# Hybrid decoder layer on one core: where weight splits and decays are computed, and in which order

## The chip, the cores and the metric

The kernel runs on one core of one Trainium2 chip. The core has a matrix engine (TensorE, PE in the profile), three engines for element-wise work (VectorE = DVE, ScalarE = ACT, GpSimd = POOL), and SyncE (SP), whose queue issues most DMA transfers. Each engine works through its own list of instructions in a fixed order and waits where an instruction's inputs or output slot are not ready. The metric is the device time of one execution in microseconds, the median over runs: 1209.37 us before the change.

## The reference

The program is one layer of a decoder, for 1024 tokens of width 1024, in float32:

```
h = rmsnorm(x); proj = h @ w_in
q,k,v (4 heads of 128) = silu(causal_conv4(proj_qkv));  q,k = l2norm(q), l2norm(k)
g = -exp(a_log) * softplus(a + dt_bias);  beta = sigmoid(b);  gc = cumsum(g)
o_a = gated delta rule over chunks (decays exp(gc_t - gc_j), triangular solve, state carried)
o_a = rmsnorm(o_a) * silu(z)
o_b = dilated sliding-window attention, 8 heads of 64, three (window, dilation) branches merged
x = x + concat(o_a, o_b) @ w_out
x = x + (silu(gate) * up) @ w_down, with gate, up = causal_conv3(rmsnorm(x) @ w_up)
return rmsnorm(x)
```

Products are computed in three passes: each float32 operand is split into a high part in TensorE's fast format and the low part that is left, and hi x hi, hi x lo and lo x hi are added up. So every weight needs a split before it is used: a copy that rounds (whi) and a subtraction (wlo = weight - whi).

## The kernel before, in words

The Python program emits instructions stream by stream. A small planner, the class `Weave` (L49), keeps a modelled clock of TensorE and of the other engines; each stream is a generator that says after how long it wants to go on, and among those that are due the one with the lowest level is taken. So the order of the products on TensorE is fixed when the program is written (`mm` stamps it, L193). On the other engines a scheduler orders the instructions: by readiness in its own timeline, and among ready ones by the order of emission. The wrappers `ve`, `ac`, `po_` (L151 to L156) emit to VectorE, ScalarE and GpSimd; `uv` and `ua` do so with a priority ahead of what was emitted before (`URGENT`). `after(inst, anchor)` (L189) adds an ordering alone. All element-wise work that goes through these wrappers has the line L142 in the profile, or L144 with priority.

`first()` computes three key heads. `dense()` (L494) then walks the rest of the input projection, one weight of 128 x 1024 after the other: the fourth key (list index 0), four plus four pieces for the values (1 to 8), then query and value tiles head by head (9 to 16), the attention's tiles (17 to 24), the gates z (25 to 28). `take()` (L512) hands out the weight for now, emits the split of the next one and the load of the one behind it. Raw weights (wst), high parts (whi) and low parts (wlo) have two slots each. `weight()` (L215) splits: those with index 1 to 8 in two halves of 512 columns with priority, the others whole and without.

`values_by_token` (L521) fills four banks with a group of the values, which ScalarE copies out into vx (L536); the next group uses the same banks. For each key, `conv_silu` (L457) runs the causal filter (a copy and a tanh on ScalarE, three filter steps and a last multiplication on VectorE), and `kprep(h)` (L598) the preparation of the delta rule: it loads the rows of gc into dec, masks them on GpSimd, takes eight exponentials on ScalarE (the decays, L613), has the key transposed into tokens and squared (`tokens`, L579, with priority on ScalarE), multiplies the key with itself and forms um from products, bp and dec (L641). From um of all keys VectorE solves small triangular systems by substitution (`forward_sub`, L684), whose blocks are merged on TensorE (`merges`); then come the chains of the four heads (`chain`), attention, output projection and the MLP. GpSimd takes powers of -0.5 and 0.5 for norms, some masks and fills, copies of reciprocals (rd), and the scaling of the heads' outputs (vtok by ms, L863).

Of the kernel before, what the change touches and what calls it, by code (L numbers as in the profile page):

```python
# [147 lines left out]
def hybrid_layer(tc, I, out):  # L148
# [23 lines left out]
    def A(name, tag, dt=F32, shape=(P, 1024)):  # L172
        if tag in TURNS:
            i = turns[tag] = turns.get(tag, -1) + 1
            tag = TURNS[tag][i % len(TURNS[tag])]
        return tile_(lp, shape, dt, name, tag, SLOTS[tag])
# [12 lines left out]
    def after(inst, anchor, reason="keeps a slot free until it is needed"):  # L189
        tc.add_manual_dep(inst.ins, anchor.ins.name, order, reason=reason)  # L190
# [9 lines left out]
    def mm3(dst, lhs, rhs, first, last, **kw):  # L200
# [2 lines left out]
        mm(dst, lhs[0], rhs[1], us, False, False, **kw)  # L203
        mm(dst, lhs[1], rhs[0], us, False, last, **kw)

    def split(src, hi, lo):
        ac.activation(hi, src, AF.Copy)
        return ve.tensor_tensor(lo, src, hi.bitcast(F32), op=OP.subtract)

    def raw_weight(src, n=1024):  # L210
# [1 line left out]
        sy.dma_start(st, src)  # L212
        return st

    def weight(src, n=1024, st=None, urgent=False):  # L215
        if st is None:
            st = raw_weight(src, n)
        hi = tile_(wp, [P, n], F32R, "whi", "whi", 2)
        lo = tile_(wp, [P, n], F32R, "wlo", "wlo", 2)
        for sl in (half(0), half(1)) if urgent else (slice(0, n),):  # L220
            (ua if urgent else ac).activation(hi[:, sl], st[:, sl], AF.Copy)
            (uv if urgent else ve).tensor_tensor(lo[:, sl], st[:, sl], hi[:, sl].bitcast(F32), op=OP.subtract)
        return hi, lo

    def wk_by_halves(src):
# [43 lines left out]
    def half(i):  # L269
        return slice(i * 512, i * 512 + 512)  # L270

    def v8(t):
        return t.rearrange("p (c t) -> p c t", c=NCH)
# [220 lines left out]
    def dense():  # L494

        yield from wv.until("first")
        yield from wv.until("norms")
        wv.add(2, first_keys())

        srcs, tiles = [], 0  # L500
        for col in DENSE:
            if col[0] == "V":
                srcs += [I["wv"][j] for j in range(4)]
            else:
                srcs.append(I["wi"][tiles])
                tiles += 1
        place = [0]
        raw = [raw_weight(srcs[0])]
        nxt = [weight(None, st=raw.pop())]
        raw.append(raw_weight(srcs[1]))  # L510

        def take():  # L512
            w = nxt.pop()
            i = place[0] = place[0] + 1
            if i < len(srcs):
                nxt.append(weight(None, st=raw.pop(), urgent=1 <= i <= 8))
            if i + 1 < len(srcs):
                raw.append(raw_weight(srcs[i + 1]))
            return w

        def values_by_token(g):  # L521

            banks = [bank(t) for t in ("asc", "asc", "ch", "ch")]
            for j in range(4):
                w = [t.rearrange("p (k m) -> p k m", k=2) for t in take()]
                for kk in range(2):
                    k = 2 * j + kk
                    for i, pt in enumerate(banks):
                        c = 4 * g + i
                        yield wv.need(pt, *w)  # L530
                        mm3(pt, [t[:, c * P:(c + 1) * P] for t in xs[k]], [t[:, kk, :] for t in w], k == 0, k == KT - 1)
            for i in range(0, 4, 2):
                vx = A("vx", "ev", shape=(P, 2, 512))
                for e in range(2):
                    c = 4 * g + i + e
                    ac.activation(vx[:, e, :], banks[i + e], AF.Copy, scale=rst[:, c:c + 1])  # L536
                c = 4 * g + i
                sy.dma_start(vpark[c * P:(c + 2) * P].rearrange("(e p) d -> p e d", e=2), vx)
            wv.done.add(("V", g))

        for i, col in enumerate(DENSE):
            kind, h = col[:2]
            if kind == "V":
                yield from values_by_token(h)
                continue
            if kind == "z":
                yield from wv.until(("o", h))
            w = [t.rearrange("p (k m) -> p k m", k=KT) for t in take()]
            pair = []
            for hh in range(2):  # L550
                pt = bank("hf")
                yield wv.need(pt, *w)
                for k in range(KT):
                    mm3(pt, [t[:, k, :] for t in w], [t[:, half(hh)] for t in xs[k]], k == 0, k == KT - 1)
                    yield 0.0

                pair.append(pt)
                if hh == 0:
                    xr = A("aqkv" if kind == "a" else "xr", "go" if kind == "k" else "ev")
                scaled(pair, "xr", kind == "a", t=xr, hs=(hh,))  # L560
            if kind == "k":
                T["k", h] = conv_silu(xr, 4 + h, "kT", "kT*")
                wv.add(3, kprep(h))
            elif kind == "q":
                q = conv_silu(xr, h, "qT", "qa")
                wv.add(4, qprep(h, q))
            elif kind == "v":
                v = conv_silu(xr, 8 + h, "vT", "qa")
                wv.add(4, vprep(h, v))
            elif kind == "z":  # L570
                og = gated[h] = A("og", "kT*")
                sy.dma_start(og, mixer[h])
                ve.tensor_tensor(og, og, silu2(xr, "zz"), op=OP.mult)
            else:
                sy.dma_start(apark[h, col[2]], xr)
                wv.done.add(col)
        wv.done.add("dense")
# [20 lines left out]
    def kprep(h):  # L598
        d = G[h]
        kT = T["k", h]  # L600
        yield from wv.until("gates")
        yield wv.need(gc)

        dec = A("dec", ("dv", "dw")[h % 2])
        gend = small("gend")
        gel = small("gel")
        rows = gdram.rearrange("(c h) t -> h c t", h=H)[h]
        sy.dma_start(v8(dec), bass.AP(tensor=rows.tensor, offset=rows.offset, ap=[[0, P]] + list(rows.ap)))
        po_.affine_select(v8(dec), v8(dec), pattern=[[0, NCH], [1, P]], compare_op=OP.is_ge, fill=NEG,
                                base=0, channel_multiplier=-1)  # L610
        late = "the rows may come later than the keys"
        after(ve.tensor_copy(gel, v8(dec)[:, :, P - 1]), kends[h][1], late)
        for c in range(NCH):  # L613
            inst = ac.activation(v8(dec)[:, c, :], v8(dec)[:, c, :], AF.Exp, bias=ngc[:, c, h:h + 1])
            after(inst, kends[h][0], late)
        ve.tensor_tensor(gend, gel, gc[:, :, h], op=OP.subtract)
        eg = small("eg")
        ac.activation(eg, gend, AF.Exp)
        ge = small("ge", 4)
        ac.activation(ge, gel, AF.Exp)  # L620
        yield wv.need(kT, slack=SLACK + 1.5 * (h == 0))
        ssk = small("ssk")
        d["ktok"] = yield from tokens(kT, A("ktok", "kt"), None, ssk)
        ve.tensor_scalar(ssk, ssk, 4.0 * EPS, None, op0=OP.add)
        nk = small("nk", 4)
        po_.tensor_tensor(nk, ssk, phalf, op=OP.pow)
        bp = small("bp", 4)
        ve.reciprocal(bp, ssk)
        ve.tensor_tensor(bp, bp, beta[:, :, h], op=OP.mult)
        ke = small("ke", 4)  # L630
        ve.tensor_tensor(ke, bp, eg, op=OP.mult)

        um = A("um", "uy", shape=(P, NCH, P))
        for c0 in range(0, NCH, 4):
            pt = yield from next_bank("atr", slack=KSLACK * (c0 == h == 0))
            for c in range(4):
                cs = slice((c0 + c) * P, (c0 + c + 1) * P)
                mm(pt[:, c * P:(c + 1) * P], kT[:, cs], kT[:, cs], 0.215)
            for c in range(4):
                i = c0 + c  # L640
                ve.scalar_tensor_tensor(um[:, i, :], pt[:, c * P:(c + 1) * P], bp[:, i:i + 1],  # L641
                                               dec[:, i * P:(i + 1) * P], op0=OP.mult, op1=OP.mult)
        md = mdram[h].rearrange("(c r) (j i) -> r j c i", r=4, j=32)
        for r in range(4):
            b = slice(32 * r, 32 * r + 32)
            sy.dma_start(md[r], um[b, :, b])
        d.update(kT=kT, dec=dec, ge=ge, nk=nk, bp=bp, ke=ke, um=um)
        wv.done.add(("k", h))
        if all(("k", i) in wv.done for i in range(H)):
            forward_sub()  # L650
# [411 lines left out]


    ots = {}
    last = {}
    x1 = {}
    MORDER = (0, 4, 1, 5, 2, 6, 3, 7)

# [576 lines left out]
```

## Time and profile before

| what | value |
|---|---|
| median of 3 runs | 1209.37 us (1208.98 to 1209.37) |
| profiled execution, its own time | 1209.18 us |
| its span, first to last instruction | 1207.4 us |
| TensorE busy | 1192.3 us (99%) |
| VectorE / ScalarE / GpSimd busy | 925.8 / 576.2 / 59.1 us |
| granted TensorE clock, mean | 0.996 |

The times in a row are microseconds from the start of the span, then the duration; ps, whi, wlo, dec, vx, um are the program's names of tiles (out<-in). A bracket at the end of a row is the idle time of the engine before it and what ended it. TensorE's products overlap, so their spacing from start to start is what counts, not the duration of one.

### The profile page before, as it was taken

What the parts mean: (1) busy time and instruction counts of PE and PEld (TensorE: products, weight loads), DVE (VectorE), ACT (ScalarE), POOL (GpSimd) and SP (SyncE); (2) the same over time, 40 slices, a digit from 0 to 9 for tenths busy, and PEclk for the clock granted to TensorE, in tenths of its full rate; (3) what the DMA queues carried; (4) which work ended last, traced back from release to release, by engine and by line L of the source; (5) the groups of instructions that cost most, each with busy time, mean ns of one, the idle gap of its engine ahead of it and who ended that gap; (6) DMA issues with size and microseconds to landing.
All of it is one profiled execution on the core that took longest, in us unless ns stands there. A gap on an engine that the chain in (4) does not pass through costs nothing.

```text
span 1207.4 us, 18350 instructions
## 1 busy us (share of the span) xinstructions
PE 1192.3 (99%) x7068; PEld 986.6 (82%) x7068; DVE 925.8 (77%) x1470; ACT 576.2 (48%) x1134; POOL 59.1 (5%) x78
## 2 busy tenths in 40 slices
PE   9999999999999999999999999999999999999997
PEld 7887888889877778888888888888888888888886
DVE  7683975666466556768988989889898889999865
ACT  7384335356355443655545445444454454444441
POOL 0211010003211000000000000000000000000000
PEclk9999999999999999999999999999999999999999
DMA  7424343435633213544223132231322298556513
GB/s 230 111 75 125 117 120 108 157 102 167 213 118 119 89 36 100 174 136 157 71 69 105 53 105 82 75 105 53 105 65 93 89 366 311 177 163 226 162 57 140
DMA packets 85798, 154.80 MB, mean 128 GB/s; under 512 B 21168, under 2 KB 36304, under 8 KB 85712
## 3 DMA queue, kind: packets, MB, share of 16 engines
q1 hardware_dynamic: 85136, 153.12, 39.3%
q8 instruction: 55, 0.90, 0.3%
q10 hardware_dynamic: 576, 0.52, 0.1%
q14 instruction: 31, 0.25, 0.1%
HBM read 117.68 MB, written 35.93 MB: 127 GB/s over the span
## 4 chain that ended last, share of the span: by engine, by line
PE 93%; DVE 3%; ACT 2%; issue 1%; DMA 1%; SPq 0%; POOLq 0%; POOL 0%; DVEq 0%; ACTq 0%
PE ps L193 44%; PE pa L193 20%; PE dw L193 17%; PE pc L193 10%; PE ps L197 3%; DVE kT L142 1%; DMA xt<-in_xT 1%; DVE wlo L142 0%; ACT dec L142 0%; DVE xr L142 0%; DVE x1h L142 0%; PE pd L193 0%; DVE qT L142 0%; SPq L142 0%; ACT xr L142 0%
## 5 line engine op out<-in xcount | busy, mean ns | idle before, releaser
L193 PE MATMUL dw<-pr 128*128 128x512 f32 (+1 forms) x984 | 211.3, 376 | 0.0
L193 PEld LDWEIGHTS dw<-pr 128*128 128x128 f32 x984 | 176.7, 188 | 33.6
L193 PE MATMUL ps<-xhi,whi 128*128 128x512 f32 x384 | 157.3, 410 | 0.0
L193 PE MATMUL ps<-xlo,whi 128*128 128x512 f32 x384 | 150.0, 391 | 0.8 <-DVE xlo L142 0.8
L193 PE MATMUL ps<-xhi,wlo 128*128 128x512 f32 x384 | 150.2, 391 | 0.0
L193 PE MATMUL pa<-T,pair 128*128 128x512 f32 x528 | 127.0, 389 | 0.0
L193 PEld LDWEIGHTS pa<-T,pair 128*128 128x128 f32 x528 | 99.0, 188 | 20.5
L193 PEld LDWEIGHTS ps<-xhi,whi 128*128 128x128 f32 x384 | 72.2, 188 | 18.1 <-issue 4.7
L193 PEld LDWEIGHTS ps<-xhi,wlo 128*128 128x128 f32 x384 | 72.1, 188 | 15.7 <-DVE wlo L142 0.2
L193 PEld LDWEIGHTS ps<-xlo,whi 128*128 128x128 f32 x384 | 72.4, 188 | 13.4 <-DVE xlo L142 1.1
L142 ACT ACTIVATE u<-pa 128x512 f32<-128x512 f32 x44 | 26.3, 598 | 107.3 <-PE pa L193 107.3
L142 DVE SCALAR_TENSOR_TENSOR y<-xu,fcw,y 128x1023 f32<-128x1023 f32 (+1 forms) x44 | 56.4, 1281 | 22.1 <-ACT y L142 22.0
L142 ACT ACTIVATE whi<-wst 128x1024 fp32r<-128x1024 f32 (+2 forms) x33 | 33.3, 1009 | 68.0 <-PE ps L193 62.4
L193 PE MATMUL pa<-B,A 128*128 128x512 f32 x264 | 63.4, 389 | 0.0
L193 PE MATMUL pc<-T,S 128*128 128x512 f32 x264 | 63.4, 389 | 0.0
L193 PE MATMUL pa<-T,S 128*128 128x512 f32 x264 | 63.4, 389 | 0.0
L193 PE MATMUL pc<-B,pair 128*128 128x512 f32 x264 | 63.4, 389 | 0.0
L142 DVE TENSOR_TENSOR wst<-wst 128x512 f32<-128x512 f32 x88 | 60.4, 687 | 0.9
L193 PE MATMUL ps<-B,pair 128*128 128x512 f32 x252 | 60.5, 389 | 0.0
L144 ACT ACTIVATE sm<-sm,mx 128x128 f32<-128x128 f32 (+7 forms) x64 | 35.4, 556 | 50.5 <-DVE mx L144 50.5
L193 PEld LDWEIGHTS pa<-T,S 128*128 128x128 f32 x264 | 49.6, 188 | 10.3
L193 PEld LDWEIGHTS pc<-T,S 128*128 128x128 f32 x264 | 49.6, 188 | 10.3
(245 smaller groups left out, 2344.7 us busy)
## 6 DMA issues: line engine op xcount, KB each, us to landing
wst<-in_wu SPq DMA_DIRECT2D x44, 512.0 KB, 3.7
wd<-in_wd SPq DMA_DIRECT2D x44, 512.0 KB, 4.5
upark<-y SPq DMA_DIRECT2D x22, 512.0 KB, 3.7
wst<-in_wi SPq DMA_DIRECT2D x21, 512.0 KB, 3.7
r<-upark SPq DMA_DIRECT2D x11, 512.0 KB, 7.5
r<-upark SPq DMA_DIRECT2D x22, 256.0 KB, 6.8
wa<-in_wd SPq DMA_DIRECT2D x22, 256.0 KB, 3.1
wst<-in_wv SPq DMA_DIRECT2D x8, 512.0 KB, 3.7
```

Source lines behind the costliest of these rows:

```text
L142: return getattr(eng, op)(*a, **kw)
L144: return getattr(eng, op)(*a, **kw)
L193: tc.stamp_issue_order_token(nc.tensor.matmul(dst, lhs, rhs, start=start, stop=stop, **kw).ins, TOKEN)
L197: tc.stamp_issue_order_token(nc.tensor.transpose(dst, src, ident if idt is None else idt).ins, TOKEN)
```

## The change

Three things are done differently.

- Weights with index 1 to 8 (the values) are split whole and without priority, through `split`, as index 0 was.
- For weights with index 9 and above in `dense()`, the high part stays on ScalarE and the low part is subtracted by GpSimd (`po_`) in place of VectorE.
- The eight decays of keys two to four (h = 1, 2, 3) are emitted behind `tokens(kT)` of that key and ordered behind the high part of the split emitted last at that point (`last["whi"]`, which `split` now records; the low parts that go to GpSimd do not pass through `split`). The first key's decays stay where they were.

```diff
+    last = {}
+
     def split(src, hi, lo):
-        ac.activation(hi, src, AF.Copy)
+        last["whi"] = ac.activation(hi, src, AF.Copy)
         return ve.tensor_tensor(lo, src, hi.bitcast(F32), op=OP.subtract)
...
-    def weight(src, n=1024, st=None, urgent=False):
+    def weight(src, n=1024, st=None, spare=False):
...
-        for sl in (half(0), half(1)) if urgent else (slice(0, n),):
-            (ua if urgent else ac).activation(hi[:, sl], st[:, sl], AF.Copy)
-            (uv if urgent else ve).tensor_tensor(lo[:, sl], st[:, sl], hi[:, sl].bitcast(F32), op=OP.subtract)
+        if spare:
+            ac.activation(hi, st, AF.Copy)
+            po_.tensor_tensor(lo, st, hi.bitcast(F32), op=OP.subtract)
+        else:
+            split(st, hi, lo)
         return hi, lo
...
-                nxt.append(weight(None, st=raw.pop(), urgent=1 <= i <= 8))
+                nxt.append(weight(None, st=raw.pop(), spare=i >= 9))
...
-        for c in range(NCH):
-            inst = ac.activation(v8(dec)[:, c, :], v8(dec)[:, c, :], AF.Exp, bias=ngc[:, c, h:h + 1])
-            after(inst, kends[h][0], late)
+
+        def decays():
+            for c in range(NCH):
+                inst = ac.activation(v8(dec)[:, c, :], v8(dec)[:, c, :], AF.Exp, bias=ngc[:, c, h:h + 1])
+                after(inst, kends[h][0], late)
+                if h:
+                    after(inst, last["whi"], "products wait for the weights first")
+
+        if h == 0:
+            decays()
...
         d["ktok"] = yield from tokens(kT, A("ktok", "kt"), None, ssk)
+        if h:
+            decays()
...
-    last = {}
```

## The prediction

> **What bounds the kernel now.** I read the page first (busy time, then the chain that ended last), then who made TensorE wait, then the stage from 60 to 101 us in time order on each engine.
>
> ```profile
> span 1207.4 us, 18350 instructions
> PE 1192.3 (99%) x7068; PEld 986.6 (82%) x7068; DVE 925.8 (77%) x1470; ACT 576.2 (48%) x1134; POOL 59.1 (5%) x78
> PE 93%; DVE 3%; ACT 2%; issue 1%; DMA 1%; SPq 0%; POOLq 0%; POOL 0%; DVEq 0%; ACTq 0%
> ```
>
> TensorE is the bound: 15.1 us of 1207.4 are idle. Nothing in this change alters the number of matrix products, so it can only win back time in which TensorE stood still or ran slowly, or add such time. Where is it? The waits of TensorE up to 500 us, longest first, and two stretches (the columns: PE, PEld, DVE, ACT and POOL busy, then the granted clock, DMA share, GB/s; the second answer was asked for TensorE alone):
>
> ```profile
> PE ps L193 <- ACT vx L142: 2.1, 1, 2.1
> PE ps L193 <- DVE wlo L144: 1.1, 1, 1.1
> 60.00:101.00 41.00, 37.79 (x189) 30.97 (x188) 27.29 (x58) 34.13 (x130) 4.91 (x3) 0.96 0.35 97
> 95.95:99.40 3.45, 3.45 (x14) 0.52 0.79 272
> ```
>
> The two longest waits inside the projections both lie between 60 and 101 us, where ScalarE is busy for 34.13 of 41 us. Behind the second wait the clock is 0.52 for 3.45 us, which loses 3.45 x 0.48 = 1.65 us more. TensorE around them:
>
> ```profile
> 67.04 0.39 PE L193 MATMUL ps<-whi,xhi 128*128 128x512 f32 x1
> 72.99 0.39 PE L193 MATMUL ps<-wlo,xhi 128*128 128x512 f32 x1
> 73.22 0.39 PE L193 MATMUL ps<-whi,xlo 128*128 128x512 f32 x1
> 73.54 0.50 PE L193 MATMUL ps<-whi,xhi 128*128 128x512 f32 x1
> 75.15 0.50 PE L193 MATMUL ps<-wlo,xhi 128*128 128x512 f32 x1 [1.11 <-DVE wlo L144]
> 92.39 0.40 PE L193 MATMUL ps<-whi,xlo 128*128 128x512 f32 x1
> 94.89 0.50 PE L193 MATMUL ps<-whi,xhi 128*128 128x512 f32 x1 [2.11 <-ACT vx L142]
> ```
>
> Products start 0.23 us apart (72.99 to 73.22). From 73.54 to 75.15 is 1.61, so 1.38 us are lost; from 92.39 to 94.89 is 2.50, so 2.27. What ScalarE and VectorE did then:
>
> ```profile
> 64.31 1.14 ACT L144 ACTIVATE whi<-wst 128x512 fp32r<-128x512 f32 x2
> 65.45 1.05 ACT L142 ACTIVATE xr<-kT 128x1024 f32<-128x1024 f32 x1
> 70.39 2.48 ACT L142 ACTIVATE dec<-dec,ngc 128x128 f32<-128x128 f32 x8
> 72.83 1.18 ACT L144 ACTIVATE whi<-wst 128x512 fp32r<-128x512 f32 x2
> 81.33 2.46 ACT L142 ACTIVATE dec<-dec,ngc 128x128 f32<-128x128 f32 x8 [2.23 <-DVE gel L142]
> 88.83 1.88 ACT L142 ACTIVATE vx<-ps,rst 128x512 f32<-128x512 f32 x3
> 90.54 1.62 ACT L142 ACTIVATE dec<-dec,ngc 128x128 f32<-128x128 f32 x5
> 92.00 1.19 ACT L144 ACTIVATE whi<-wst 128x512 fp32r<-128x512 f32 x2
> 93.05 1.02 ACT L142 ACTIVATE dec<-dec,ngc 128x128 f32<-128x128 f32 x3
> 94.12 0.71 ACT L142 ACTIVATE vx<-ps,rst 128x512 f32<-128x512 f32 x1
> 70.57 3.92 DVE L142 SCALAR_TENSOR_TENSOR kT<-xr,gcw,kT 128x1023 f32<-128x1023 f32 x3 [0.23 <-ACT kT L142]
> 74.41 1.29 DVE L144 TENSOR_TENSOR wlo<-wst,whi 128x512 fp32r<-128x512 f32 x2
> 89.81 2.15 DVE L142 SCALAR_TENSOR_TENSOR um<-ps,bp,dec 128x128 f32<-128x128 f32 x8
> ```
>
> At 70.39 the eight decays of the second key run before the high part of the third value weight (72.83), though the slot of that weight was free from 67.04 on, when the second weight took over on TensorE. At 90.54 to 94.1 the decays of the fourth key stand between the third and the fourth copy (vx) that empty the value banks, and TensorE waits for the fourth. So both waits trace back to decays that nobody needs yet.
>
> **The change part by part.**
>
> *Decays of keys two to four behind their transposes and behind a split.* 24 instructions move, none goes; a key's eight take 2.48 us. Second key: out of the way at 70.39, the high part can start 2.44 us earlier (72.83 - 70.39). The wait of 1.38 can go whole; the least is nothing, since VectorE is held by three steps of the keys' filters until 74.41 and the low part may still follow them. Fourth key: the fourth copy can follow the third at about 90.6 instead of 94.12, so 2.27 and, with it, the slow clock of 1.65. Cover on the consumers' side: the decays are read by the products' evacuation into um, which for the second key begins at 89.81, 19 us after they ran; I cost that at nothing (without that cover it would be 2.5 us per key). What is late next: the copies vx may now meet the third key's eight, which move from 81.33, where ScalarE had been idle for 2.23, to behind its transposes, close to 88; if all eight go first, up to 2.48 us. Between 0 and 2.48 I take 0.6, since the one row of such a meeting (90.54) let three copies go first. Queues: SP's loads of weights stay bound to the low parts, which come earlier or at the same time here; no DMA moves.
>
> *Weights two to nine split whole and without priority.* For each, 2 x 0.6 on ScalarE and 2 x 0.68 on VectorE become one instruction each:
>
> ```profile
> L142 DVE TENSOR_TENSOR wlo<-wst,whi x28: 557/1224/1425, 4.3 to 476.9; 128x1024 fp32r<-128x1024 f32 x23, 128x768 fp32r<-128x768 f32 x3, 128x384 fp32r<-128x384 f32 x2
> L144 DVE TENSOR_TENSOR wlo<-wst,whi x18: 679/684/694, 32.0 to 498.9; 128x512 fp32r<-128x512 f32 x18
> L142 ACT ACTIVATE whi<-wst x21: 1041/1062/1122, 115.6 to 464.9; 128x1024 fp32r<-128x1024 f32 x21
> ```
>
> The first half is usable after 1.06 + 1.22 = 2.28 us instead of about 0.6 + 0.68 = 1.3: 1 us later. Where engines are free (the weights from 101 us on) the split is done several microseconds before use: nothing. For the second weight the low part was done at about 66.2, used from 67.04; whole, behind the high part from 64.31, it ends at 64.31 + 2.28 = 66.6: just in time, but 0.8 to 2.0 late if the tanh (xr, 1.05 us) goes first. Third and fourth weights: at most one filter step of 1.31 us each (3.92 / 3). Ends 0 and 4.6; I take 1.4 us for all, nearer the low end, because ScalarE and VectorE lose nothing in total and gain 2.5 us of room per moved key.
>
> *The low parts of the last 20 projection weights on GpSimd.* VectorE loses 20 x 1.22 = 24.5 us, GpSimd gains 20 subtractions. The nearest rows, and the contention:
>
> ```profile
> L142 POOL TENSOR_TENSOR vtok<-vtok,ms x4: 1897/1897/1898, 288.6 to 314.6; 128x1024 f32<-128x1024 f32 x4
> L142 POOL TENSOR_SCALAR_AFFINE_SELECT dec<-dec x4: 1252/1394/2022, 50.9 to 56.2; 128x1024 f32<-128x1024 f32 x4
> 51.74 7.59 DVE L142 SCALAR_TENSOR_TENSOR kT<-xr,gcw,kT 128x1023 f32<-128x1023 f32 x4
> 263.89 0.38 PE L193 MATMUL ps<-ct,qat 128*128 128x128 f32 x1 [0.27 <-DVE vtok L144]
> PE ps L193 <- DVE pb L144: 0.3, 2, 0.2
> L142 DVE SCALAR_TENSOR_TENSOR kT<-xr,gcw,kT x12: 1275/1282/2103, 49.9 to 83.5; 128x1023 f32<-128x1023 f32 x4, 128x1022 f32<-128x1022 f32 x4, 128x1021 f32<-128x1021 f32 x4
> L142 POOL TENSOR_TENSOR ms<-ms,mhalf 128x8 f32<-128x8 f32 x4 | 6.5, 1636 | 12.3 <-DVE ms L142 12.3
> L193 PE MATMUL ps<-x,um x192: 184/200/267, 193.5 to 221.0; 32*32 32x32 f32 x128, 64*64 64x64 f32 x64
> L142 SPq DMA_DIRECT2D um<-xtdram x16: 432/449/1341, 170.0 to 180.4; - x16
> ```
>
> One takes 1.9 us, at most 1.9 x 2.02 / 1.25 = 3.1 when VectorE is in the way. A weight's 48 products last 48 x 0.23 = 11 us, and the split starts when the weight before last is done, so 1.06 + 3.1 is hidden by 11; without that cover it would cost 0.7 to 1.9 per weight. VectorE pays: four filter steps took 7.59 us beside the selects against 4 x 1.31 = 5.24, so 2.35 us for some 6 us of GpSimd, 0.74 per subtraction against 1.22 saved. The place where VectorE sets a date is the substitution (120 to 165 us), whose blocks are loaded by about 183 (last issue 180.4) and first multiplied at 193.5: 10 us of slack. What TensorE can win is small: 0.27 at 263.89 (a low part stood before vtok) and 0.3 in two waits for pb in attention, together 0.6; I take 0.5. Queued behind a subtraction on GpSimd are the powers of the norms and the copies of reciprocals: at most 1.9 us each, filled by TensorE's other streams; I take nothing, and 4 us for the case below.
>
> Here a page speaks against the change: the Trainium skill, SBUF — State Buffer, section "Who interferes with whom", says that a VectorE instruction with two SBUF inputs and a GpSimd instruction that reads SBUF exclude each other, the second one blocked entirely. The trace agrees (filter steps of 2.10 beside the selects, 1.28 otherwise). By that rule each of five subtractions in the substitution costs 1.9 - 1.22 = 0.7 us, 3.5 in all, still within 10: the sum stays.
>
> Sum: 1.38 + 2.27 + 1.65 + 0.5 won, 0.6 + 1.4 lost: 3.8 us. The profiled execution took 1209.18 (span 1207.4 and 1.8 around it), so 1205.4; the median of the runs is 0.2 above it, 1205.6.
>
> **The rivals.**
>
> *Half of it is given back (no change).* The third key's decays go before all four copies: TensorE meets the same wait of about 2 us at about 89 us, and the slow clock with it, and 1.38 + 0.5 less 1.4 remain: 0.5 us won, 1208.9. For it: those decays are emitted before the copies. Against: ScalarE has room before the copies, as it no longer runs the fourth key's.
>
> *Splits without priority come late (slower).* The filter steps and tanh of the keys, emitted earlier, go ahead of weights two, three and four: 2.0 + (1.38 + 0.6) + 2.0 of waits, two of them followed by a slow clock of 1.65: 9.3 us, where 5.3 were lost before: 4 us slower, 1213.4. It decides once the splits' delays exceed the 5.3 that the moved decays free. For it: VectorE at 70.57 to 74.41 already shows filters ahead of a low part that had priority.
>
> *GpSimd becomes late (slower).* Four powers and four scalings of the heads' outputs (1.6 and 1.9 us) at 287 to 316 queue with low parts; if attention starts 1.9 us late twice: 1213.
>
> *The slow clock is not of the wait.* The Trainium skill, TensorE: Matmul & The Clock Gate, section "Why this matters for your kernels", puts the drop at idle gaps above about 3 us; here 2.1 us of waiting precede it, so the trace says less is needed. If the drop came anyway, 3.8 - 1.65 = 2.1 us would be won: 1207.2.
>
> **How the numbers follow.** A measurement of this kernel tells about 0.2% (2.4 us) from no change. Forecast 0.46 (faster, own range 1203.5 to 1206.9); half given back 0.17 and clock not of the wait 0.06 (within 0.2%); splits late 0.23 and GpSimd late 0.08 (slower). So faster 0.46, same 0.23, slower 0.31. The low end is all that can be won, 1.38 + 2.27 + 1.65 + 0.6 = 5.9 us with nothing given back: 1203.5; the high end the two slow cases, 1213.4.
>
> **What would show it.** Right: between 60 and 101 us no wait for wlo or vx above 0.6 us and a clock of 1.00; the decays of key four after 95 us; 20 subtractions of about 2 us on GpSimd with no TensorE wait on them. Wrong: new waits for whi or wlo at weights two to four, a clock below 1 there, or waits on GpSimd between 280 and 330 us.

## The result, and the profile after

The changed kernel takes 1205.85 us (median of 10 runs, 1204.28 to 1207.41), the kernel before beside it 1208.28 (1206.73 to 1209.37). The ratio is 0.9978, 95% interval 0.9970 to 0.9986: 2.7 us less. The forecast was 1205.6, or 3.8 us less than the 1209.37 it started from; beside the changed kernel the kernel before took 1.1 us less than that. The profiled execution took 1206.67 us with a span of 1204.6.

The page of the kernel after, its span, busy times and the chain's shares:

```profile
span 1204.6 us, 18326 instructions
PE 1191.6 (99%) x7068; PEld 987.0 (82%) x7068; DVE 916.1 (76%) x1442; ACT 575.3 (48%) x1126; POOL 108.2 (9%) x98
PE 93%; DVE 4%; ACT 1%; issue 1%; DMA 1%; SPq 0%; POOLq 0%; POOL 0%; DVEq 0%; ACTq 0%
```

GpSimd has 20 more instructions and 49.1 us more of busy time, 47.9 of it in the subtractions. TensorE is idle for 13.0 us of the span in place of 15.1. Where did idle time go, and where did it come from? First the waits of TensorE between 60 and 175 us in the kernel after, the longest first:

```profile
PE ps L197 <- DVE at L142: 1.6, 1, 1.6
PE ps L193 <- DVE xr L142: 0.5, 1, 0.5
PE ps L197 <- DVE gq L142: 0.3, 1, 0.3
```

The waits for wlo and vx are gone, and three new ones, for results of VectorE, have come. The windows of the kernel after (columns as in the prediction: PE, PEld, DVE, ACT, POOL, clock, DMA share, GB/s); the third row was asked for TensorE alone:

```profile
60.00:101.00 41.00, 41.00 (x217) 34.67 (x216) 29.69 (x62) 29.25 (x100) 4.92 (x3) 1.00 0.38 109
120.00:170.00 50.00, 47.52 (x220) 38.62 (x219) 44.68 (x90) 17.39 (x36) 11.35 (x5) 0.97 0.30 108
...
153.40:156.90 3.50, 3.41 (x10) 0.52 0.37 150
```

The second of these windows in the kernel before:

```profile
120.00:170.00 50.00, 50.00 (x241) 41.89 (x240) 44.21 (x95) 19.75 (x40) 3.61 (x3) 1.00 0.37 128
```

From 60 to 101 us TensorE now has no idle time and a full clock: the prediction's 1.38 + 2.27 + 1.65 are all won. From 120 to 170 us, where before nothing was lost, 2.48 us are idle and the clock is 0.52 for 3.5 us. A table of stages shows the same, each time taken from the start of one product to that of another in the profiled executions (value weights: first product of two high parts with them to the last such; then to the first merge of the substitution's blocks; to the first scores of attention; to the first product of the MLP):

| us | before | after |
|---|---|---|
| the value weights | 59.48 | 54.06 |
| to the first merge | 73.31 | 77.07 |
| to the first scores | 133.58 | 133.66 |
| to the MLP | 236.48 | 235.00 |

5.4 us are won in the first stage, 3.8 given back in the second, 1.5 won in attention.

What ScalarE did in the stage that was won, in time order in the kernel after:

```profile
74.92 1.06 ACT L142 ACTIVATE whi<-wst 128x1024 fp32r<-128x1024 f32 x1 [4.00 <-issue]
75.89 2.44 ACT L142 ACTIVATE dec<-dec,ngc 128x128 f32<-128x128 f32 x8
86.46 0.69 ACT L142 ACTIVATE vx<-ps,rst 128x512 f32<-128x512 f32 x1 [2.09 <-PE ps L193]
87.15 2.05 ACT L142 ACTIVATE vx<-ps,rst 128x512 f32<-128x512 f32 x3
90.04 1.56 ACT L142 ACTIVATE dec<-dec,ngc 128x128 f32<-128x128 f32 x5
103.08 2.14 ACT L142 ACTIVATE dec<-dec,ngc 128x128 f32<-128x128 f32 x7
```

The high part goes ahead of the second key's decays (74.92, 75.89); the four copies vx go ahead of the third key's (87.15, then 90.04), so the meeting for which the prediction took 0.6 us did not happen; the fourth key's eight are at 103, where no copy waits.

Now the stage that gives back. GpSimd's subtractions there, VectorE beside them and TensorE behind, all in the kernel after (three views: GpSimd's, VectorE's and TensorE's timeline):

```profile
127.64 2.53 POOL L142 TENSOR_TENSOR wlo<-wst,whi 128x1024 fp32r<-128x1024 f32 x1 [7.73 <-ACT whi L142]
140.88 2.50 POOL L142 TENSOR_TENSOR wlo<-wst,whi 128x1024 fp32r<-128x1024 f32 x1 [10.71 <-ACT whi L142]
```

```profile
127.54 0.38 DVE L142 TENSOR_TENSOR xi<-xi,tmp 128x207 f32<-128x207 f32 x1
127.95 2.46 DVE L142 TENSOR_TENSOR tmp<-mt,xi 128x220 f32<-128x220 f32 x1
...
141.02 0.68 DVE L142 TENSOR_TENSOR xr<-ps,rstdB 128x512 f32<-128x512 f32 x1
141.62 2.04 DVE L142 TENSOR_TENSOR xi<-xi,tmp 128x255 f32<-128x255 f32 x1
...
152.31 1.12 DVE L142 SCALAR_TENSOR_TENSOR at<-ps,bp,dec 128x128 f32<-128x128 f32 x4
```

```profile
138.17 0.47 PE L193 MATMUL ps<-xhi,whi 128*128 128x512 f32 x1 [0.50 <-DVE xr L142]
...
151.30 0.63 PE L197 MATMUL ps<-ident,vT 128*128 128x128 f32 x4 [0.29 <-DVE gq L142]
153.49 1.10 PE L197 MATMUL ps<-ident,vT 128*128 128x128 f32 x4 [1.56 <-DVE at L142]
```

A step of the substitution takes about 0.4 us (0.38 at 127.54). The one that begins while GpSimd subtracts takes 2.46, and the next time 2.04; each ends 0.2 to 0.3 us after GpSimd's instruction (130.41 and 143.66 against 130.17 and 143.38). An evacuation that began inside GpSimd's second instruction and has one operand in ps, the accumulators (141.02), took 0.68 as everywhere. So it is the steps with both operands in SBUF (the memory of the program's tiles outside ps) that stand still, about 2.1 and 1.6 us longer here. On VectorE's list the evacuations into xr and at stand behind those steps, and TensorE waits for them. (The wait that the profile puts down to gq belongs with these: gq is an instruction of 0.16 us right behind four evacuations into at, at 151.07.)

### The profile page after: what moved, and what is told of

Same layout as the page of the kernel before. It is cut to its first block, busy times and chain, and to the rows that moved or that the text cites. A ratio compares the mean times of both kernels' runs of the same rounds, so it can differ in the third digit from the quotient of the medians.

```text
span 1204.6 us, 18326 instructions
## 1 busy us (share of the span) xinstructions
PE 1191.6 (99%) x7068; PEld 987.0 (82%) x7068; DVE 916.1 (76%) x1442; ACT 575.3 (48%) x1126; POOL 108.2 (9%) x98
## 4 chain that ended last, share of the span: by engine, by line
PE 93%; DVE 4%; ACT 1%; issue 1%; DMA 1%; SPq 0%; POOLq 0%; POOL 0%; DVEq 0%; ACTq 0%
PE ps L193 43%; PE pa L193 20%; PE dw L193 17%; PE pc L193 10%; PE ps L197 3%; DVE tmp L142 1%; DVE xi L142 1%; PE warm L193 1%; ACT sm L144 0%; DMA mt<-mdram 0%; DVE xr L142 0%; DVE qT L142 0%; DVE vT L142 0%; DMA mdram<-um 0%; DVE x1h L142 0%
## 5 line engine op out<-in xcount | busy, mean ns | idle before, releaser
L142 ACT ACTIVATE whi<-wst 128x1024 fp32r<-128x1024 f32 (+2 forms) x41 | 41.8, 1019 | 72.1 <-PE ps L193 40.3
L142 POOL TENSOR_TENSOR rs<-rs,mhalf 128x2 f32<-128x2 f32 (+2 forms) x4 | 4.5, 1116 | 738.7 <-DVE rs L144 738.7
L144 ACT ACTIVATE sm<-sm,mx 128x128 f32<-128x128 f32 (+7 forms) x64 | 35.4, 555 | 47.9 <-DVE mx L144 47.9
L142 POOL TENSOR_TENSOR wlo<-wst,whi 128x1024 fp32r<-128x1024 f32 x20 | 47.9, 2393 | 115.6 <-ACT whi L142 113.7
```

Source lines behind the costliest of these rows:

```text
L142: return getattr(eng, op)(*a, **kw)
L144: return getattr(eng, op)(*a, **kw)
```

## The experiments

Each is compared with the kernel before on the same chip; the ratio's 95% interval is in brackets. All of them compute the whole layer. Two questions: what is each of the three parts worth, and is it GpSimd that gives back?

### The change without GpSimd, and GpSimd alone

The first is the kernel after with this edit:

```diff
-                nxt.append(weight(None, st=raw.pop(), spare=i >= 9))
+                nxt.append(weight(None, st=raw.pop(), spare=False))
```

> The changed kernel with all low parts on VectorE; whole splits and moved decays stay. Theory (GpSimd's subtractions hold up the steps of the substitution by about 2 us each, and that makes TensorE wait near 150 us): no wait above 0.5 us for at or gq between 135 and 160 us, clock 1.00 there, 60 to 101 us as clean as in the changed kernel; about 2.5 us faster than the changed kernel, ratio to the kernel before about 0.996. Rival (TensorE only meets VectorE there because it runs some 5 us earlier than before): the wait of about 1.6 us near 150 us stays, ratio about 0.998.

The second is the kernel before, with halves, priority and decays as they were, and the low parts of index 9 and above on GpSimd:

```diff
-                nxt.append(weight(None, st=raw.pop(), urgent=1 <= i <= 8))
+                nxt.append(weight(None, st=raw.pop(), urgent=1 <= i <= 8, spare=i >= 9))
```

> The kernel before with the low parts of weights 9 and above on GpSimd, nothing else. Theory: the waits for wlo near 75 and vx near 95 us stay with the slow clock; steps of the substitution that meet a subtraction take 2.0 to 2.5 us instead of 0.4, so a new wait of TensorE between 125 and 165 us is possible; ratio 1.000 to 1.002. Rival (TensorE being early is what makes the wait): no new wait between 125 and 165 us, the small waits behind low parts near 264, 306, 354 and 383 us go, ratio about 0.9995.

Without GpSimd: 0.9965 [0.9952, 0.9977], 1204.66 against 1208.8 us. GpSimd alone: 1.0006 [0.9997, 1.0015], no difference. The window of the change without GpSimd:

```profile
120.00:170.00 50.00, 50.00 (x243) 41.88 (x242) 45.31 (x97) 19.11 (x52) 2.92 (x2) 1.00 0.30 109
```

and the window, the waits and one VectorE row of GpSimd alone:

```profile
120.00:170.00 50.00, 47.09 (x220) 38.14 (x219) 45.46 (x86) 16.86 (x37) 14.37 (x7) 1.00 0.42 124
```

```profile
PE ps L193 <- ACT sq L144: 1.3, 1, 1.3
PE ps L197 <- DVE at L142: 1.1, 1, 1.1
```

```profile
132.18 2.50 DVE L142 TENSOR_TENSOR tmp<-mt,xi 128x255 f32<-128x255 f32 x1
```

The wait for sq is of the same kind, by way of ScalarE: another step was held from 145.34 for 2.51 us, xr followed it on VectorE at 147.78, the tanh vT on ScalarE waited 3.35 us for xr (148.49), and the squares sq stand behind that tanh.

The rival to GpSimd as the cause was that TensorE, some 5 us earlier than before, simply comes before VectorE is ready. It falls: without GpSimd TensorE is nearly as early and waits for nothing in this window; with GpSimd alone TensorE is only 0.9 us early and waits. Product by product the lists of TensorE in the change and in the change without GpSimd are the same from 105 to 192 us, so the lag can be read at each: -0.90 us at 105, 0.33 at 139.91 (behind the wait for xr), 2.58 at 153.49 (behind those for gq and at; a group of eight transposes is also broken in two there), 4.23 at 157.2 (the slow clock), 4.25 at 192. So 3.5 us came with the three waits and 1.65 with the slow clock behind them. GpSimd alone against the kernel before goes from -0.94 to 3.12 in the same stretch, all in waits.

The -0.90 at the start is a miss of what was expected: without GpSimd the stage from 60 to 101 us is not as clean as in the change. TensorE waits there 0.76 us for sq at 68.20 (the kernels with GpSimd from index 14 and 15 on have such a wait as well), because ScalarE is 0.9 us later, and that begins at the keys' filters: four steps of VectorE beside GpSimd's selects took 7.60 us in this profile and 6.76 in the change. The selects begin at other times there (53.25 and 55.10 against 53.57 on); why is not shown.

Why is GpSimd alone no slower, then? Its stages are 77.36, 132.46 and 235.05 us against 73.31, 133.58 and 236.48: 4.1 lost between the value weights and the merges, 2.5 won behind them. (The first stage is 58.69 against 59.48.)

### Which of GpSimd's subtractions cost, and which win

Two kernels made of the one after:

```diff
-                nxt.append(weight(None, st=raw.pop(), spare=i >= 9))
+                nxt.append(weight(None, st=raw.pop(), spare=i >= 14))
```

> The changed kernel with GpSimd taking low parts only from weight 14 on, so that the substitution (120 to 165 us) meets one or none. Theory (its steps being held up causes the wait near 150 us): that wait goes, ratio to the kernel before about 0.996, as without GpSimd or slightly better, since the small waits behind low parts near 264, 306, 354 and 383 us stay away. Rival (TensorE being early causes it): the wait stays, ratio about 0.998.

```diff
-                nxt.append(weight(None, st=raw.pop(), spare=i >= 9))
+                nxt.append(weight(None, st=raw.pop(), spare=9 <= i < 14))
```

> The changed kernel with GpSimd taking the low parts of weights 9 to 13 only, those that fall into and just before the substitution; the later ones on VectorE. Theory (these five do the harm, the other fifteen are worth some 2 us): three steps of the substitution stretched to 2.0 to 2.5 us, a wait for at of 1 to 2 us near 150 us with a slow clock behind it; ratio about 0.999, slower than the whole change and than no subtraction on GpSimd at all. Rival (the harm and the gain are chance of the order): ratio 0.9965, as without GpSimd.

From index 14 on: 0.9945 [0.9932, 0.9957], 1202.24 us, the lowest median of all kernels here: its five runs (1201.85 to 1203.21) all lie below the five without GpSimd (1204.24 to 1205.53) on the same chip, though the two intervals of the ratio overlap a little. Index 9 to 13 only: 0.9988 [0.9980, 0.9997]. Against the change without GpSimd (0.9965) the later subtractions win 0.0020, some 2.4 us, and the first five cost 0.0023, some 2.8 us. Both together would give 0.9968; the change has 0.9978, with an interval that ends at 0.9970. With some 0.001 of uncertainty in each ratio, that is no contradiction; whether the five cost more in the whole change than alone is not shown. A TensorE row of the profile of index 9 to 13 and the window behind that row:

```profile
151.75 0.66 PE L197 MATMUL ps<-ident,vT 128*128 128x128 f32 x4 [1.51 <-DVE at L142]
```

```profile
151.70:155.20 3.50, 3.45 (x17) 1.00 0.37 150
```

Here a wait of 1.51 us is followed by a full clock; in the change one of 1.56 was followed by 0.52. This profile, however, is of the fastest of the eleven runs (1205.60 us, median 1207.24), and in it TensorE is only 0.90 us behind the change without GpSimd from 152 us on (-0.83 before the wait). So it shows the wait, but not all of the 2.8 us. The clock is not what sets the other runs apart: most have the same mean of 0.998.

From index 14 on, the window and GpSimd's first subtraction:

```profile
120.00:170.00 50.00, 50.00 (x243) 41.93 (x242) 45.28 (x95) 19.11 (x52) 4.20 (x2) 1.00 0.31 109
```

```profile
164.66 2.45 POOL L142 TENSOR_TENSOR wlo<-wst,whi 128x1024 fp32r<-128x1024 f32 x1 [18.40 <-ACT whi L142]
```

It begins at 164.66, near the end of the substitution; TensorE's list and times up to 192 us are those of the change without GpSimd, to 0.1 us.

And the win behind the merges? The prediction counted 0.27 for vtok and 0.3 for two waits for pb. One of these two places in the kernel before, then the same place in the kernel after (TensorE's timeline; both end with the next product of the projection):

```profile
353.72 0.48 PE L193 MATMUL ps<-kT,qT 64*128 64x128 f32 x2
354.37 1.42 PE L193 MATMUL ps<-kT,qT 64*128 64x128 f32 x6 [0.17 <-DVE pb L144]
355.73 0.50 PE L193 MATMUL ps<-xhi,whi 128*128 128x512 f32 x1
```

```profile
351.63 0.93 PE L193 MATMUL ps<-kT,qT 64*128 64x128 f32 x8
352.49 0.50 PE L193 MATMUL ps<-xhi,whi 128*128 128x512 f32 x1
```

The eight small products take 355.73 - 353.72 = 2.01 us from start to start where the third has to wait, and 0.86 where it does not. The bracket says 0.17; the place costs 1.15. The trace's single starts say where the rest goes. Each of these products uses 64 of the 128 rows. Without the wait they start in pairs 0.007 us apart (351.633 and 351.640, 351.846 and 351.853, and so on), so two run side by side; in the kernel before they start one at a time, 0.10 to 0.44 us apart (353.719, 353.932, 354.374 and on). The second place (382.72 to 384.74, 2.02 us, before; 379.71 to 380.56 after) costs as much. Both are broken in the change without GpSimd and whole in the change and from index 14 on, and so it is with the wait for vtok, whose place takes 2.12 us from start to start before (263.23 to 265.35) and 1.52 after (262.75 to 264.27). Twice 1.15 and 0.60 are 2.9 us, against some 2.4 measured.

### The decays alone, and the whole splits alone

The kernel before with its halves and priority, the decays moved as in the change, no GpSimd:

```diff
         for sl in (half(0), half(1)) if urgent else (slice(0, n),):
-            (ua if urgent else ac).activation(hi[:, sl], st[:, sl], AF.Copy)
+            last["whi"] = (ua if urgent else ac).activation(hi[:, sl], st[:, sl], AF.Copy)
...
+        if h:
+            decays()
```

> The kernel before with the decays of keys two to four moved as in the change (ordered behind the last high part of any weight); splits of weights 1 to 8 keep halves and priority, all low parts on VectorE. Theory (the moved decays carry the gain): both waits and the slow clock between 60 and 101 us go, about 5 us won, ratio about 0.996. Rival (the whole splits without priority are needed as well, since halves with priority push other work back): a wait of 1 us or more stays between 60 and 101 us, ratio 0.998 or more.

The kernel before with whole splits, decays in their old place, no GpSimd:

```diff
-                nxt.append(weight(None, st=raw.pop(), urgent=1 <= i <= 8))
+                nxt.append(weight(None, st=raw.pop(), urgent=False))
```

> The kernel before with the value weights split whole and without priority; decays where they were, all low parts on VectorE. Theory (the moved decays alone carry the gain, the form of the splits is worth nothing): the waits near 75 and 95 us and the slow clock stay, ratio 0.9995 to 1.002. Rival (the form of the splits carries part of the gain): one of the waits goes, ratio 0.998 or less.

Decays alone: 0.9964 [0.9951, 0.9976], the same as with whole splits on top (0.9965). Whole splits alone: 0.9976 [0.9967, 0.9985], a win where a loss was expected. The windows of the two, decays alone first:

```profile
60.00:101.00 41.00, 40.97 (x217) 34.53 (x216) 30.02 (x68) 30.04 (x106) 5.29 (x3) 1.00 0.38 110
```

```profile
60.00:101.00 41.00, 39.48 (x208) 32.58 (x207) 30.12 (x62) 34.83 (x127) 7.78 (x6) 1.00 0.35 98
```

ScalarE's timeline with whole splits alone shows why they win by themselves:

```profile
69.96 2.47 ACT L142 ACTIVATE dec<-dec,ngc 128x128 f32<-128x128 f32 x8
72.51 1.07 ACT L142 ACTIVATE whi<-wst 128x1024 fp32r<-128x1024 f32 x1
...
87.65 1.33 ACT L142 ACTIVATE vx<-ps,rst 128x512 f32<-128x512 f32 x2
88.79 2.51 ACT L142 ACTIVATE dec<-dec,ngc 128x128 f32<-128x128 f32 x8
91.33 1.32 ACT L142 ACTIVATE vx<-ps,rst 128x512 f32<-128x512 f32 x2
```

In the kernel before the third copy ended at 90.7 and the fourth began at 94.12, with five decays, two halves of a high part that had priority, and three decays in between. Here the eight decays run in one piece with no split among them, and the last copies begin at 91.33, so the long wait and the slow clock behind it are gone. The decays ahead of the high part at 69.96 stay, and with them the wait for wlo at 75.25 (1.11 us) and one of 0.40 for whi before it (39.48 of 41 busy). Both parts thus remove the long wait, and their gains do not add: 0.0024 and 0.0036 alone, 0.0035 together.

### Halves, and GpSimd from the next weight on; and the change once more

The decays-alone kernel with GpSimd from index 15:

```diff
-                nxt.append(weight(None, st=raw.pop(), urgent=1 <= i <= 8))
+                nxt.append(weight(None, st=raw.pop(), urgent=1 <= i <= 8, spare=i >= 15))
```

> Moved decays; value weights split in halves with priority as before; GpSimd takes low parts from weight 15 on, so that the substitution meets none. Theory (moved decays win 4 to 5 us, the later subtractions on GpSimd 2 to 3, the form of the splits nothing): ratio 0.994 to 0.995, as with GpSimd from 14 and whole splits. Rival (whole splits are needed for the best): 0.996 or more.

0.9955 [0.9942, 0.9969], 1202.99 us: with whole splits and GpSimd from 14 it was 0.9945 with an interval that overlaps this one. So neither the halves nor one subtraction more makes a difference that these runs can tell.

The change itself again, with no edit:

> The changed kernel itself once more, beside the others on the same chip: ratio 0.9978 as measured, wait for at near 150 us.

0.9977 [0.9967, 0.9987], 1205.67 us. Its lag against the change without GpSimd goes from -1.10 at 105 us to 3.05 at 154.3, with waits of 1.56 for at, 0.28 for gq and two of about 0.5 for xr. So these waits came in both profiled executions of the kernel. The slow clock did not. The window behind the wait of 1.56 (it ends at 153.91 here), asked for TensorE alone:

```profile
153.80:157.30 3.50, 3.39 (x17) 1.00 0.37 150
```

The same products behind the same wait thus ran at a clock of 0.52 in one execution and at 1.00 in the other. The first took 1206.67 us, the second 1205.62.

## Why the prediction was right, and where its steps were not

That the time came out 0.25 us from the forecast is luck in two ways. The gain was 2.7 us and not 3.8, and the kernel before, measured beside the change, was 1.1 us faster than the 1209.37 from which the forecast was taken off. And the gain itself is a sum of two errors of opposite sign: what the first two parts win was forecast at 3.3 us and is 4.2 (0.9965); what GpSimd does was forecast as 0.5 won and is about 1.6 lost (0.9978 against 0.9965, whose intervals overlap a little). None of the prediction's signs of being wrong came: they looked at the value weights and at 280 to 330 us, and the loss lay between.

- **Decays of the second and fourth key** (1.38 + 2.27 + 1.65): as forecast. Both waits and the slow clock are gone wherever the decays were moved. By the Trainium skill's page TensorE: Matmul & The Clock Gate, section "Why this matters for your kernels", the drop belongs to idle gaps above about 3 us. The rows differ: a clock of 0.52 stands behind waits of 2.11 and 1.56 us, but not behind one of 1.51, and not behind the same 1.56 in the second profile of the change. So less than 3 us can be enough and does not have to be, and the 1.65 is what one profiled execution lost; how many of the timed runs lose it is not shown. The rival that the clock would stay slow anyway falls: in the profiles of the change, of its parts and of the kernels without the wait for vx the clock from 60 to 101 us is 1.00; in the one that keeps that wait (GpSimd alone) it is 0.96, each in one execution.
- **The third key's decays meeting the copies** (0.6): cost nothing; all four copies went first.
- **Whole splits** (1.4 lost): on top of moved decays they cost nothing (0.9965 with, 0.9964 without), alone they win 2.9 us. The step overlooked that a high part with priority is itself something that can stand between two copies: the rows at 92.00 and 94.12 that the prediction quotes showed it.
- **Price of a subtraction on GpSimd** (1.9, at most 3.1): 2.35 to 2.53 us, median 2.38. The row that it was taken from, vtok by ms, was not near enough.
- **What VectorE pays for one** (0.74 against 1.22 saved): mis-sized. A substitution step that meets a subtraction is held for 1.6 to 2.1 us, so in the substitution VectorE loses where it was to gain. The price came from filter steps beside selects on GpSimd; they were slowed to 2.10 at most. They too were held until the select ended (one began at 53.17, the select ended at 54.20, the step at 55.27), so what they lost depended on when they began, and was no price for other meetings. Later subtractions hold filter steps as well (2.34 to 2.48 us at 170, 185 and 196 us in the change, where one takes 1.28 alone), and there TensorE does not wait. The Trainium skill's rule that the prediction weighed (SBUF — State Buffer, "Who interferes with whom": the second of the two is blocked entirely) describes what these rows show, and so does its other half, that a VectorE instruction with at most one input in SBUF does not contend (0.68 at 141.02).
- **"10 us of slack"**: this is the step that failed, for the prediction also weighed 3.5 us of contention and put it at nothing because of this slack. It is true for the merges, which TensorE did not wait for, and beside the point. The slack was taken at the last reader of the substitution. VectorE's list in that stretch also holds the evacuations xr and at, which TensorE waited for (0.50 and 1.56 us), and VectorE had little room there. Its busy time from 126 to 156 us in the kernel before (asked for VectorE alone):

```profile
126.00:156.00 30.00, 28.16 (x61) 1.00 0.25 81
```

That is 28.16 of 30 us. Of the prediction's two bounds for the contention, 3.5 us against 10 of slack, the 3.5 is what TensorE lost in waits, and the 10 did not cover it. That the figures agree is chance: the 3.5 was five meetings at 0.7 us, and three steps were met and held for 1.6 to 2.1.
- **GpSimd's later subtractions** (0.5 of 0.6 won): about 2.4 won. The places were right (vtok and two times pb); the size was read from the idle brackets and not from the spacing, and the pairs that a wait breaks up were not seen.
- **GpSimd late for the heads' outputs** (a rival at 280 to 330 us): did not come; the place where GpSimd hurt was the substitution.

## What to carry to other kernels

When work is moved to GpSimd, look at what VectorE runs at that time, operand by operand: here a short instruction with two inputs in SBUF was held for the rest of GpSimd's instruction (2.46 us in place of 0.4), and everything behind it on VectorE's list was late with it, so slack has to be taken at the first reader of that list and not at the last. Move the work only in stretches where VectorE runs other forms or where TensorE does not wait for what stands behind; here that choice alone was worth 4 us (0.9945 against 0.9978). Before a slow clock is put down to a wait, take a second profile: one execution can have it and the next not. And price a wait in a group of small products by the spacing from start to start, with and without it, not by the idle time in the bracket.

## What the runs showed of the hardware

- A wait of 0.17 us within eight products of 64 rows cost 1.15 us: with it 2.01 from start to start, one product at a time; without it 0.86, in pairs that start 0.007 us apart.
- The subtraction of 128x1024 took 2.38 us on GpSimd (median of 20) where VectorE takes 1.22, and this with little spread (2.35 to 2.53) even where it met VectorE. In those meetings it was VectorE that waited. The Trainium skill (GPSIMD Engine Reference, "4.1 Engine selection") puts two-input work at about twice VectorE's time, and the rows agree.
- The clock fell to 0.52 for 3.5 us behind a wait of 1.56 us, and stayed at 1.00 behind the same wait in another execution of the same kernel, and behind one of 1.51 in another kernel. What decides it no run here shows.
